# Decoder layer on one core: GpSimd's scaling and adding handed to VectorE, 16 bias adds made one, the last pair's weight sums moved into the up projection

## The chip, the cores and the metric

The kernel runs on one core of a Trainium2 chip. The metric is the device time of one execution in microseconds (us). The five engines of the core run their own instruction queues in order: TensorE (PE in the profile; its weight loads are PEld), VectorE (DVE), ScalarE (ACT), GpSimd (POOL) and SyncE (SP), which here only issues DMAs. Engines wait for each other through semaphores.

## The reference

One post-norm decoder layer in float32: 512 tokens, 1024 channels, 8 + 8 attention heads of 64, 2816 channels in the gated MLP. Cut to what matters here:

```python
mod = c @ w_ada + b_ada                      # six vectors of 1024
sh1, sc1, gt1, sh2, sc2, gt2 = split(mod, 6)
u = x * (1.0 + sc1) + sh1
q_a, k_a, v_a, f_a, q_b, k_b, v_b, g_a, g_b = split(u @ w_in)
y_fox = forgetting_attention(q_a, k_a, v_a, log_sigmoid(f_a + b_forget))
y_sb = stick_breaking_attention(q_b, k_b, v_b)
merged = sigmoid(g_a) * (y_fox @ w_fox_proj) + sigmoid(g_b) * (y_sb @ w_sb_proj)
x = layer_norm(ALPHA * x + (1.0 + gt1) * (merged @ w_o), ln1_g, ln1_b)
u2 = x * (1.0 + sc2) + sh2
h_gate, h_val = split(causal_depthwise_conv(u2 @ w_up, conv_w, conv_b), 2)
x = layer_norm(ALPHA * x + (1.0 + gt2) * ((silu(h_gate) * h_val) @ w_down), ln2_g, ln2_b)
```

## The kernel before

**Numbers.** Every large product is made in three matmuls of a float32 form (`wh*ah + wh*al + wl*ah`): an operand `r` is split into a rounded high part (`hi_of`, a copy on ACT, line 89) and the rest (`lo_of`, a subtraction on DVE, line 92). So each weight tile of 128x1024 costs an ACT copy and a DVE subtraction (`wl`, two inputs in SBUF) before PE can use it.

**The stream of weights.** `items` is one list of weight loads in the order of use. `weights(i)` issues loads through SP up to five items ahead (`LOADS = 5` buffers called `raw`) and runs each item's `proc` up to some items ahead of its use; the split products `wh`/`wl` have three buffers (`WBUFS = 3`). A load can start only when the last reader of its `raw` buffer is done. The order of instructions on all engines but SP is set by a scheduler at build time from this program order; SP's order is as written.

**Stages.** To 190 us: the first projections and the attention pairs, with the loads of `w_ada` in between (`ada_proc`). A `w_ada` block of 128x1024 is multiplied by `c` and summed along its row by one DVE instruction with an accumulator (`mod_sum`, line 201), and a bias is added to the one resulting column (`mod_col`, line 207, 128x1): `n` from 8 to 23 are the shift and scale of the MLP, which are first read at lines 845 to 847 (`gm`, `bm`, at 338 us). From about 244 to 345 us: the branch projections (`bproj`), the gates and the loads of `w_o`. `merge` adds the two gated branch sums on GpSimd (line 738, 128x512, eight times), and `wo_proc` multiplies each `w_o` block by `1 + gt1` on GpSimd (line 634, 128x1024, eight times) ahead of the split. From 345 to 372 us: the output projection and the first layer norm.

**Up projection and MLP** (372 to 674 us). 44 column blocks `n` of `w_up`, 24 matmuls of 512 columns each; after every fourth one, a pair `p = 0..10` of 256-channel groups of the hidden layer is complete. The down projection is a Strassen-Winograd scheme over 2x2 blocks, seven products per pair: the DVE makes sums of the activations (`blocks`, lines 1063 to 1066) and of the weights (`pair_proc`). For a pair, `raw` B is loaded (columns 0 to 1023 of `wdp[p]`) and columns 512 to 1535 are added to it by a GpSimd DMA; then the sums R are loaded (columns 1024 to 2047) and DVE makes `wg = R[0:512]*g` (line 946), `R[0:512] += B[0:512]` (947), `R[512:] += R[0:512]` (948), splits both halves of R (`wdc_proc`: `wdh`, `wdl`) and scales B by `g` (951). B goes to DRAM in `t13[p]`, `wg` in `wgt[p]`, both issued by ACT, and are loaded again in the phases after the up projection. `early_products(p)` makes three of the products with the halves of `wdp[p]` and the sums R; it stands behind block `n = 4p + 7`, for the last two pairs behind block 43 and in `z_mark`. `ready(p)` splits another sum of the activations into halves `hv` (two ACT copies and two DVE subtractions of 128x256); it is called in the up projection for the first `GS = 9` pairs and in `z_mark` for the rest.

**The last pair** (`p = 10`) is outside this pattern: its B, its halves and R are loaded behind the first Z load, its sums are made after block 43, B isn't stored but split from SBUF (`state["t13"]`), and `phase` uses that split in a special case (`last`).

**After the up projection:** four phases of products over the eleven pairs, Z (`zi`: `t13[p]` columns 512 to 1023), V (`vi`: `t13[p]` columns 0 to 511), X (`xi`) and W (`wi`, `cli`), each with two PSUM banks and with layer-norm work on DVE between them, then the tail.

Of the kernel before, what the change touches and what calls it, by code (L numbers as in the profile page):

```python
# [16 lines left out]
P = 128  # L17
# [25 lines left out]
GS = 9  # L43
# [8 lines left out]
def layer_kernel(ctx: ExitStack, tc: tile.TileContext, out, xT, x, cT, crow, wa0, wa1, bcol, bgt, w1, wct, wv, bf,  # L52
# [6 lines left out]
    t13 = [tc.dram_tile([P, 1024], F32, name=f"t13_{p}") for p in range(FP - 1)]  # L59
    wgt = [tc.dram_tile([P, 512], F32, name=f"wgt_{q}") for q in range(FP)]  # L60
    st1 = ExitStack()
# [571 lines left out]
    def wo_proc(r):  # L633
        G.tensor_tensor(r, r, gt[0], ALU.mult)  # L634
# [101 lines left out]
    def merge(j):  # L736
        def f(m):
            G.tensor_tensor(m, m, ma[j], ALU.add)
# [105 lines left out]
    bm = const([P, KT], F32, "bm")  # L844
    V.scalar_tensor_tensor(gm, lnc[:, 0, :], -0.5, modc[:, 3, :], ALU.mult, ALU.mult)
# [95 lines left out]
    def pair_proc(p):  # L941
        def f(r):
# [25 lines left out]
    wui, pi, wai = [], [], {}  # L968

    def add_pair_items(p):  # L970
        pi.append([add_item(wdp[p][:, 0:1024], raw_proc)])
        items[-1].append(wdp[p][:, 512:1536])
        pi[p].append(add_item(wdp[p][:, 0:512], halves_proc))

    def add_pair_sums(p):
        pi[p].append(add_item(wdp[p][:, 1024:2048], pair_proc(p)))

    for n in range(2 * FT):
# [206 lines left out]
    def phase(ps, idx, end, take, mark, last=None, fresh=True):  # L1185
# [7 lines left out]
        if end < FP:  # L1193
            t = take(end)
            for i in range(2):
                product(ps[i], t[:, top[i]], t[:, bot[i]], *[v[last] for v in state["t13"]], False, True)
            mark(len(idx))
# [57 lines left out]
    phase(Z, zi, FP - 1, g_part(0), z_mark, 1)  # L1255
    W1 = [bank() for _ in range(2)]
    phase(W1, vi, FP - 1, g_part(1), v_mark, 0)
# [100 lines left out]
```

## Time and profile before

| | us |
|---|---|
| median of 3 runs (lowest, highest) | 751.56 (750.51, 752.71) |
| profiled execution: time | 750.47 |
| profiled execution: span on the core | 748.7 |
| PE busy | 734.3 (98%) |
| DVE busy | 607.9 (81%) |
| ACT busy | 389.0 (52%) |
| POOL busy | 111.1 (15%) |

The profiled execution lasted 1.77 us longer than its span and 1.09 us less than the median of the runs. PE's granted clock is full over the whole span. A PE row's duration contains the drain of the matmul, so that a matmul of 512 columns shows 0.39 us while the next one starts after 0.23; a true stall is read from the start of one matmul to the start of the next. In the rows, an engine's idle time stands in square brackets with what ended it.

### The profile page before, as it was taken

The numbers are of one execution on the slowest core, as the hardware profiler recorded it, in microseconds if no ns is written. First come the engines' busy times: TensorE is split into PE (matmuls) and PEld (weight loads), VectorE is DVE, ScalarE is ACT, GpSimd is POOL, SyncE is SP. The second block draws the span as 40 slices with busy tenths as digits, with TensorE's granted clock in tenths as the row PEclk, the third lists the DMA queues.
The fourth block names the chain that finished last, engine by engine and source line by source line (L and its number), as shares of the span: only waits on it lengthen the run. The fifth ranks groups of instructions, "written<-read, shape, count | busy, mean of one in ns | idle before, by whom it ended". The sixth has DMA issues, their size and how long they took to land.

```text
span 748.7 us, 9890 instructions
## 1 busy us (share of the span) xinstructions
PE 734.3 (98%) x3478; PEld 608.1 (81%) x3478; DVE 607.9 (81%) x1018; ACT 389.0 (52%) x682; POOL 111.1 (15%) x140
## 2 busy tenths in 40 slices
PE   8999999999999999999999999999999999999995
PEld 4878888878888888788889888888888888887885
DVE  6869799888788795756577899988888696668996
ACT  4566465685876564443055455444454454436550
POOL 1026223353000011444000000000000000000010
PEclk9999999999999999999999999999999999999999
DMA  8943545413412230552052788577787574666734
GB/s 330 406 179 113 169 170 190 148 58 113 170 62 109 93 133 28 197 200 87 1 205 93 219 294 263 165 221 231 255 283 224 179 213 146 203 169 209 241 90 94
DMA packets 44244, 130.11 MB, mean 174 GB/s; under 512 B 5761, under 2 KB 6273, under 8 KB 44194
## 3 DMA queue, kind: packets, MB, share of 16 engines
q1 hardware_dynamic: 37890, 112.61, 43.1%
q0 software_dynamic: 2992, 7.93, 6.1%
q10 hardware_dynamic: 3312, 8.93, 3.2%
q8 instruction: 27, 0.44, 0.2%
q14 instruction: 23, 0.19, 0.1%
HBM read 117.59 MB, written 11.80 MB: 173 GB/s over the span
## 4 chain that ended last, share of the span: by engine, by line
PE 86%; DVE 7%; DMA 3%; ACT 2%; issue 2%; POOL 0%; SPq 0%; DVEq 0%; ACTq 0%
PE ps L136 18%; PE ps L134 18%; PE ps L135 18%; PE ps L302 5%; PE ps L1084 4%; PE ps L1082 4%; PE ps L1083 4%; PE ps L553 2%; PE ps L535 2%; PE ps L895 2%; PE ps L893 2%; PE ps L894 2%; DVE wl L92 1%; PE ps L476 1%; PE ps L477 1%
## 5 line engine op out<-in xcount | busy, mean ns | idle before, releaser
L92 DVE TENSOR_TENSOR wl<-raw,wh 128x1024 fp32r<-128x1024 f32 (+2 forms) x112 | 139.0, 1242 | 39.5 <-ACT wh L183 39.1
L183 ACT ACTIVATE wh<-raw 128x1024 fp32r<-128x1024 f32 (+1 forms) x103 | 108.3, 1052 | 108.2 <-PE ps L135 50.7
L134 PE MATMUL ps<-u2h,wh 128*128 128x512 f32 (+1 forms) x376 | 141.4, 376 | 0.0
L135 PE MATMUL ps<-u2l,wh 128*128 128x512 f32 (+1 forms) x376 | 141.2, 376 | 0.0
L136 PE MATMUL ps<-u2h,wl 128*128 128x512 f32 (+1 forms) x376 | 141.2, 375 | 0.0
L136 PEld LDWEIGHTS ps<-u2h,wl 128*128 128x128 f32 x376 | 70.8, 188 | 12.9
L135 PEld LDWEIGHTS ps<-u2l,wh 128*128 128x128 f32 x376 | 70.8, 188 | 12.8
L134 PEld LDWEIGHTS ps<-u2h,wh 128*128 128x128 f32 x376 | 70.8, 188 | 12.7
L134 PE MATMUL ps<-uh,wh 128*128 128x512 f32 x200 | 79.5, 397 | 0.0
L136 PE MATMUL ps<-uh,wl 128*128 128x512 f32 x200 | 78.3, 391 | 0.9 <-DVE wl L92 0.9
L135 PE MATMUL ps<-ul,wh 128*128 128x512 f32 x200 | 78.3, 391 | 0.0
L1132 ACT ACTIVATE cv<-ps,cw 128x512 f32<-128x512 f32 x44 | 34.0, 773 | 39.9 <-PE ps L136 30.7
L1133 DVE SCALAR_TENSOR_TENSOR cv<-ps,cw,cv 128x511 f32<-128x511 f32 x44 | 32.7, 744 | 15.6 <-ACT cv L1132 15.6
L136 PEld LDWEIGHTS ps<-uh,wl 128*128 128x128 f32 x200 | 37.6, 188 | 9.5 <-DVE wl L92 1.3
L515 POOL TENSOR_TENSOR pt<-pt,om 128x127 f32<-128x127 f32 (+3 forms) x32 | 43.2, 1361 | 8.0 <-DVE om L514 8.0
L134 PEld LDWEIGHTS ps<-uh,wh 128*128 128x128 f32 x200 | 37.6, 188 | 7.3
L135 PEld LDWEIGHTS ps<-ul,wh 128*128 128x128 f32 x200 | 37.6, 188 | 7.2
L162 POOL DMA_DIRECT2D raw<-in_wdp x11 | 9.6, 869 | 192.6 <-DVE raw L948 67.3
L1134 DVE SCALAR_TENSOR_TENSOR cv<-ps,cw,cv 128x510 f32<-128x510 f32 x44 | 32.7, 743 | 0.3
L1140 ACT ACTIVATE cv<-cv 128x512 f32<-128x512 f32 x22 | 13.9, 631 | 36.0 <-DVE cv L1134 36.0
L634 POOL TENSOR_TENSOR raw<-raw,gt 128x1024 f32<-128x1024 f32 x8 | 20.5, 2562 | 67.6 <-DMA raw<-in_wo 55.1
L514 DVE TENSOR_TENSOR_SCAN om<-om,dg 128x127 f32<-128x127 f32 (+3 forms) x32 | 29.6, 981 | 0.5 <-ACT om L509 0.4
(227 smaller groups left out, 1613.8 us busy)
## 6 DMA issues: line engine op xcount, KB each, us to landing
raw<-in_wup SPq DMA_DIRECT2D x44, 512.0 KB, 4.7
raw<-in_wa SPq DMA_DIRECT2D x32, 512.0 KB, 4.2
raw<-in_wct SPq DMA_DIRECT2D x25, 512.0 KB, 3.7
raw<-in_wdp SPq DMA_DIRECT2D x22, 512.0 KB, 5.4
wa<-in_wa SPq DMA_DIRECT2D x14, 512.0 KB, 7.6
raw<-in_wdp SPq DMA_DIRECT2D x22, 256.0 KB, 4.4
raw<-in_wdp POOLq DMA_DIRECT2D x11, 512.0 KB, 7.5
t<-raw ACTq DMA_DIRECT2D x10, 512.0 KB, 3.0
```

The costliest lines, as they stand in the source:

```text
L92: state["read"] = V.tensor_tensor(o, i, fl(hi), ALU.subtract)
L134: PE.matmul(ps, wh, ah, start=first, stop=False)
L135: PE.matmul(ps, wh, al, start=False, stop=False)
L136: return PE.matmul(ps, wl, ah, start=False, stop=last)
L183: state["hi"] = S.activation(h[:, 0:cols], r[:, 0:cols], AF.Copy)
L302: PE.matmul(grp[g], w, u, start=j == 0 and n == 0, stop=j == KT - 1 and n == (1 if g == 7 else 2))
L515: G.tensor_tensor(pt[b][:, s : e - 1], pt[b][:, s : e - 1], om[:, s + 1 : e], ALU.mult)
L1082: PE.matmul(ps, ah, bh, start=first, stop=False, skip_group_check=onto)
L1083: PE.matmul(ps, ah, bl, start=False, stop=False, skip_group_check=onto)
L1132: S.activation(t, ps, AF.Identity, bias=cw[:, n, 3:4], scale=cw[:, n, 2:3])
L1133: V.scalar_tensor_tensor(t[:, 1:], ps[:, 0:511], cw[:, n, 1:2], t[:, 1:], ALU.mult, ALU.add)
L1134: V.scalar_tensor_tensor(t[:, 2:], ps[:, 0:510], cw[:, n, 0:1], t[:, 2:], ALU.mult, ALU.add)
```

## The change

Four things are edited. (1) `ada_proc` calls only `mod_sum` for `n` from 8 to 23, so that the 16 one-column adds of line 207 are gone; one 128x16 add in front of `gm` (line 846 of the changed kernel) makes all 16 columns at once. (2) The eight multiplications of `wo_proc` and the eight additions of `merge` are issued on VectorE instead of GpSimd. (3) The last pair's B and R are loaded and summed as items behind blocks 31 and 32 of the up projection. R isn't split there but stored to a new DRAM tile `t24`, and B is stored to `t13[10]`; after the up projection the halves of `wdp[10]` and `t24` are loaded and split behind the first Z load, and `t13[10]` is the eleventh entry of the Z and V phases, whose special case goes. (4) `GS` is 7 instead of 9: `ready(7)` and `ready(8)` are called in `z_mark`.

```diff
-GS = 9
+GS = 7
...
-    t13 = [tc.dram_tile([P, 1024], F32, name=f"t13_{p}") for p in range(FP - 1)]
+    t13 = [tc.dram_tile([P, 1024], F32, name=f"t13_{p}") for p in range(FP)]
+    t24 = tc.dram_tile([P, 1024], F32, name="t24")
...
             if 8 <= n < 24:
-                mod_col(2 + (n - 8) // 8, n % 8, r)
+                mod_sum(2 + (n - 8) // 8, n % 8, r, slice(0, D), 0)
                 return
...
     def wo_proc(r):
-        G.tensor_tensor(r, r, gt[0], ALU.mult)
+        V.tensor_tensor(r, r, gt[0], ALU.mult)
...
         def f(m):
-            G.tensor_tensor(m, m, ma[j], ALU.add)
+            V.tensor_tensor(m, m, ma[j], ALU.add)
...
+    V.tensor_tensor(modc[:, 2:4, :], modr[:, 2:4, :, 0], bcols[:, 2:4, :], ALU.add)
     V.scalar_tensor_tensor(gm, lnc[:, 0, :], -0.5, modc[:, 3, :], ALU.mult, ALU.mult)
...
-            w = wdc_proc(r)
+            w = wdc_proc(r) if p < FP - 1 else None
...
             with tc.issue_after(state["last"].ins):
-                if p < FP - 1:
-                    S.dma_start(t13[p], b)
+                S.dma_start(t13[p], b)
                 if p > 1:
                     S.dma_start(wgt[p], g)
-            if p == FP - 1:
-                state["t13"] = wdc_proc(b)
+                if p == FP - 1:
+                    S.dma_start(t24, r)
             return w
...
+        if n == 31:
+            add_pair_items(FP - 1)
+        if n == 32:
+            add_pair_sums(FP - 1)
...
-    for p in range(0, FP - 1, 2):
-        add_two(zi, lambda q: t13[q][:, 512:1024], p, FP - 1)
+    for p in range(0, FP, 2):
+        add_two(zi, lambda q: t13[q][:, 512:1024], p, FP)
         if p == 0:
-            add_pair_items(FP - 1)
-            add_pair_sums(FP - 1)
-    for p in range(0, FP - 1, 2):
-        add_two(vi, lambda q: t13[q][:, 0:512], p, FP - 1)
+            pi[FP - 1].append(add_item(wdp[FP - 1][:, 0:512], halves_proc))
+            pi[FP - 1].append(add_item(t24, wdc_proc))
+    for p in range(0, FP, 2):
+        add_two(vi, lambda q: t13[q][:, 0:512], p, FP)
```

The order of the instructions, at the three places of which the prediction speaks. First VectorE in the attention stage, from the scans `om` of the stick-breaking branch to the forget gate's row `fq`; `m` and `pl` are low parts of attention operands, `wl` of a weight tile. Before:

```order
L514 SCALAR_TENSOR_TENSOR om_1582<-om_1582,dg 128x511
L92 TENSOR_TENSOR wl_1618<-raw_1609,wh_1617 128x1024
L207 TENSOR_TENSOR modc<-modr,bcols 128x1
L92 TENSOR_TENSOR m_0_553<-ps_1528,m_300_1597 64x512
L92 TENSOR_TENSOR m_1_554<-ps_1528,m_301_1600 64x512
L92 TENSOR_TENSOR pl_1633<-ps_1627,ph_1632 128x512
L92 TENSOR_TENSOR pl_1641<-ps_1636,ph_1640 128x384
L92 TENSOR_TENSOR ptc_544<-ps_1644,ptc_543 128x384
L359 SCALAR_TENSOR_TENSOR fq_571<-fq_571,fq_570 8x512
L360 SCALAR_TENSOR_TENSOR fq_570<-ones,fq_571 8x512
```

and in the changed kernel:

```order
L515 SCALAR_TENSOR_TENSOR om_1580<-om_1580,dg 128x511
L93 TENSOR_TENSOR wl_1616<-raw_1607,wh_1615 128x1024
L93 TENSOR_TENSOR m_0_555<-ps_1527,m_300_1595 64x512
L93 TENSOR_TENSOR m_1_556<-ps_1527,m_301_1598 64x512
L93 TENSOR_TENSOR pl_1631<-ps_1625,ph_1630 128x512
L93 TENSOR_TENSOR pl_1639<-ps_1634,ph_1638 128x384
L93 TENSOR_TENSOR ptc_546<-ps_1642,ptc_545 128x384
L360 SCALAR_TENSOR_TENSOR fq_573<-fq_573,fq_572 8x512
L361 SCALAR_TENSOR_TENSOR fq_572<-ones,fq_573 8x512
L93 TENSOR_TENSOR wl_1682<-raw_1609,wh_1681 128x1024
```

The 128x1 add between `wl` and `m` is gone, and nothing else moves.

Second VectorE where the branch sums (`sg`, `ml`), the `w_o` blocks (`woh`, `wol`) and the gates' weights (`wl`) meet. Before:

```order
L207 TENSOR_TENSOR modc<-modr,bcols 128x1
L628 TENSOR_TENSOR sg_2948<-ps_3117,sg_2948 128x512
L92 TENSOR_TENSOR wl_3150<-raw_3139,wh_3149 128x1024
L92 TENSOR_TENSOR ml_3133<-sg_2948,mh_3132 128x512
L92 TENSOR_TENSOR wl_3194<-raw_3180,wh_3193 128x1024
L92 TENSOR_TENSOR wol_3187<-raw_3141,woh_3185 128x512
L92 TENSOR_TENSOR wl_3230<-raw_3216,wh_3229 128x1024
L92 TENSOR_TENSOR wol_3188<-raw_3141,woh_3186 128x512
L628 TENSOR_TENSOR sg_3021<-ps_3179,sg_3021 128x512
L92 TENSOR_TENSOR ml_3212<-sg_3021,mh_3211 128x512
```

and in the changed kernel, where L739 is the branch sum, L635 the scaling of a `w_o` block and L846 the one bias add:

```order
L846 TENSOR_TENSOR modc<-modr,bcols 128x16
L629 TENSOR_TENSOR sg_2937<-ps_3104,sg_2937 128x512
L93 TENSOR_TENSOR wl_3136<-raw_3126,wh_3135 128x1024
L739 TENSOR_TENSOR sg_2937<-sg_2937,sg_653 128x512
L635 TENSOR_TENSOR raw_3128<-raw_3128,gt_1210 128x1024
L93 TENSOR_TENSOR ml_3120<-sg_2937,mh_3119 128x512
L93 TENSOR_TENSOR wl_3180<-raw_3166,wh_3179 128x1024
L635 TENSOR_TENSOR raw_3168<-raw_3168,gt_1210 128x1024
L93 TENSOR_TENSOR wol_3173<-raw_3128,woh_3171 128x512
L93 TENSOR_TENSOR wl_3216<-raw_3202,wh_3215 128x1024
L93 TENSOR_TENSOR wol_3174<-raw_3128,woh_3172 128x512
L629 TENSOR_TENSOR sg_3009<-ps_3165,sg_3009 128x512
```

A branch sum and two scalings now stand in VectorE's queue there, the first of them between `wl_3136` and `ml_3120`.

Third the last pair. SyncE's loads around blocks 32 to 35 of the up projection, before:

```order
L157 DMA raw_5587<-in_wup 128x1024
L157 DMA raw_5589<-in_wup 128x1024
L157 DMA raw_5591<-in_wup 128x1024
L157 DMA raw_5635<-in_wdp 128x1024
L157 DMA raw_5638<-in_wdp 128x512
L157 DMA raw_5698<-in_wup 128x1024
L157 DMA raw_5744<-in_wdp 128x1024
L157 DMA raw_5807<-in_wup 128x1024
L157 DMA raw_5809<-in_wup 128x1024
L157 DMA raw_5811<-in_wup 128x1024
```

and in the changed kernel, where `raw_5576` is B of the last pair and `raw_5623` its R:

```order
L158 DMA raw_5574<-in_wup 128x1024
L158 DMA raw_5576<-in_wdp 128x1024
L158 DMA raw_5579<-in_wup 128x1024
L158 DMA raw_5623<-in_wdp 128x1024
L158 DMA raw_5625<-in_wup 128x1024
L158 DMA raw_5693<-in_wdp 128x1024
L158 DMA raw_5696<-in_wdp 128x512
L158 DMA raw_5738<-in_wup 128x1024
L158 DMA raw_5740<-in_wdp 128x1024
L158 DMA raw_5801<-in_wup 128x1024
L158 DMA raw_5803<-in_wup 128x1024
L158 DMA raw_5805<-in_wup 128x1024
```

Each of the two stands between loads of `w_up`, so that the `w_up` blocks behind them take `raw` buffers that come free later. VectorE after block 43, before, from the last pair's first weight sum to the halves `hv` for its early products:

```order
L946 TENSOR_TENSOR wg_6383<-raw_6273,gt_4554 128x512
L92 TENSOR_TENSOR wl_6442<-raw_6380,wh_6441 128x1024
L947 TENSOR_TENSOR raw_6273<-raw_6273,raw_6235 128x512
L92 TENSOR_TENSOR wl_6479<-raw_6405,wh_6478 128x1024
L948 TENSOR_TENSOR raw_6273<-raw_6273 128x512
L92 TENSOR_TENSOR wdl_6389<-raw_6273,wdh_6387 128x512
L951 TENSOR_TENSOR raw_6235<-raw_6235,gt_4554 128x512
L92 TENSOR_TENSOR wdl_6390<-raw_6273,wdh_6388 128x512
L92 TENSOR_TENSOR wl_6507<-raw_6438,wh_6506 128x1024
L92 TENSOR_TENSOR wdl_6399<-raw_6235,wdh_6397 128x512
L92 TENSOR_TENSOR wdl_6400<-raw_6235,wdh_6398 128x512
L92 TENSOR_TENSOR hv_6432<-cv_6162,hv_6432 128x256
```

and in the changed kernel:

```order
L93 TENSOR_TENSOR wl_6387<-raw_6370,wh_6386 128x1024
L1074 TENSOR_TENSOR sg_1191_6359<-cv_6150,cv_6253 128x256
L93 TENSOR_TENSOR wl_6412<-raw_6373,wh_6411 128x1024
L93 TENSOR_TENSOR fo_6365<-cv_6150,fh_6364 128x256
L93 TENSOR_TENSOR fo_6365<-cv_6253,fh_6364 128x256
L93 TENSOR_TENSOR hv_6402<-cv_6150,hv_6402 128x256
L93 TENSOR_TENSOR hv_6405<-cv_6253,hv_6405 128x256
L93 TENSOR_TENSOR hv_6445<-sg_1062_5687,hv_6445 128x256
L93 TENSOR_TENSOR hv_6448<-sg_1062_5687,hv_6448 128x256
L93 TENSOR_TENSOR wl_6455<-raw_6376,wh_6454 128x512
```

The four sums of lines 946 to 951 and the four `wdl` are gone from there (two `wdl` of `t24` stand earlier), and the halves `hv_6445` and `hv_6448` of pair 7 (`ready`) have come in.

More of the change, by code (lines that the diff above doesn't have):

```diff
@@ L966, in scale_proc @@
         return f
-    wui, pi, wai = [], [], {}
+    wui, pi, wai = [], [[] for _ in range(FP)], {}
     def add_pair_items(p):
-        pi.append([add_item(wdp[p][:, 0:1024], raw_proc)])
+        pi[p].append(add_item(wdp[p][:, 0:1024], raw_proc))
         items[-1].append(wdp[p][:, 512:1536])
-        pi[p].append(add_item(wdp[p][:, 0:512], halves_proc))
+        if p < FP - 1:
+            pi[p].append(add_item(wdp[p][:, 0:512], halves_proc))
     def add_pair_sums(p):
-        pi[p].append(add_item(wdp[p][:, 1024:2048], pair_proc(p)))
+        n = add_item(wdp[p][:, 1024:2048], pair_proc(p))
+        if p < FP - 1:
+            pi[p].append(n)
     for n in range(2 * FT):
@@ L1183, in layer_kernel, with phase @@
     p1, u2, q1, u3, tm = [[fine(n) for _ in range(2)] for n in ("p1", "u2", "q1", "u3", "tm")]
-    def phase(ps, idx, end, take, mark, last=None, fresh=True):
+    def phase(ps, idx, end, take, mark, fresh=True):
         for n, k in enumerate(idx):
@@ L1192, in phase @@
             mark(n)
[L1193 to L1197, printed above, removed]
     def g_part(c):
@@ L1254, in layer_kernel @@
     Z = [bank() for _ in range(2)]
-    phase(Z, zi, FP - 1, g_part(0), z_mark, 1)
+    phase(Z, zi, FP, g_part(0), z_mark)
     W1 = [bank() for _ in range(2)]
-    phase(W1, vi, FP - 1, g_part(1), v_mark, 0)
+    phase(W1, vi, FP, g_part(1), v_mark)
     phase(P1, xi, FP, lambda p: ops[p][1], x_mark, fresh=False)
```

## The prediction

> **What bounds the kernel now.** I read the page's first part, then PE's waits, then a table by stage (after the span: busy time and count of PE, PEld, DVE, ACT and POOL, then PE's clock, DMA share and GB/s), and last the timeline around each wait. All numbers are of the one profiled execution: 750.47 us, which is 748.7 of span and 1.77 around it, and 1.09 below the median of 751.56.
>
> ```profile
> PE 734.3 (98%) x3478; PEld 608.1 (81%) x3478; DVE 607.9 (81%) x1018; ACT 389.0 (52%) x682; POOL 111.1 (15%) x140
> ...
> PE ps L553 <- DVE m L92: 0.9, 1, 0.9
> PE ps L136 <- DVE wl L92: 0.9, 1, 0.9
> PE ps L1084 <- DVE hv L92: 0.6, 1, 0.6
> ...
> 293.00:316.00 23.00, 22.12 (x100) 17.88 (x99) 16.23 (x19) 11.43 (x17) 8.65 (x4) 1.00 0.45 161
> 316.00:365.00 49.00, 49.00 (x218) 40.55 (x217) 28.16 (x37) 15.23 (x24) 18.50 (x10) 1.00 0.32 110
> 540.00:610.00 70.00, 70.00 (x311) 57.93 (x310) 55.63 (x89) 34.27 (x55) 3.16 (x4) 1.00 0.69 221
> 666.00:693.00 27.00, 25.75 (x109) 19.70 (x108) 22.39 (x37) 15.10 (x26) 0.00 (x0) 1.00 0.55 188
> 693.00:735.00 42.00, 42.00 (x188) 34.76 (x188) 39.30 (x67) 20.63 (x30) 3.51 (x4) 1.00 0.59 159
> ```
>
> PE is the bound: 98% busy at full clock (the 1.00). So work that is added to DVE or taken from POOL changes nothing by itself; only PE's stalls do, and they are few and short. In 540 to 610 us 311 matmuls fill 70.00 us, 0.225 each; at that pace the 109 matmuls of 666 to 693 need 24.5 of the 27.00, so about 2.5 us are lost there. The three waits in the list are the three places that the change touches.
>
> **Part 1, the 16 adds.** First PE's rows at the stall of line 553 and at the next one, then DVE's, ACT's, and two pieces of the chain of waits between them:
>
> ```profile
> 157.67 0.39 PE L453 MATMUL ps<-wh,ul 128*128 128x512 f32 x1
> 158.95 0.65 PE L553 MATMUL ps<-ph,vv 128*128 128x512 f32 x2 [0.89 <-DVE m L92]
> ```
>
> ```profile
> 186.25 0.52 PE L535 MATMUL ps<-ident,pt 128*128 128x128 f32 x3 [0.37 <-DVE vv L92]
> ```
>
> ```profile
> 156.36 1.04 DVE L207 TENSOR_TENSOR modc<-modr,bcols 128x1 f32<-128x1 f32 x1
> 157.41 1.39 DVE L92 TENSOR_TENSOR m<-ps,m 64x512 fp32r<-64x512 f32 x2
> ...
> 160.42 0.68 DVE L359 SCALAR_TENSOR_TENSOR fq<-fq,fq 8x512 f32<-8x512 f32 x1
> ```
>
> ```profile
> 159.76 0.63 ACT L358 ACTIVATE fq<-fq 8x512 f32<-8x512 f32 x1
> ```
>
> ```profile
> 163.49 3.36 DMA raw<-in_wa
> ...
> 173.94 4.45 DMA raw<-in_wa
> ```
>
> The 128x1 add takes 1.04 us here, in front of the `m` for which PE waits. Without it `m` starts 1.04 earlier, and PE's 1.28 from start to start (157.67 to 158.95) falls to the pace of 0.23: the stall of 1.05 goes. But what is late next? ACT's `fq` ends at 160.39, and DVE's line 359, which reads it, started at 160.42: from there on DVE keeps its old times, whatever it gained. The next weight tile frees the buffer for the load issued at 163.49, whose block is summed before the scans; these and the next tile set the load at 173.94; its sum stands before the `vv` for which PE waits at 186.25. The chain from 160 to 186 runs over DVE and two loads and not over PE, so PE arrives 1.05 earlier at 186.25 and waits there. What remains is the adds on that chain and the 0.03 at `fq`, one or two adds of 0.07 to 0.16 as rows: I take −0.2. The bounds are 0 and −1.05 (the chain moves with PE). The new 128x16 add has 16 times the columns of an add that is nearly all fixed cost; it runs once, at about 306 us, and counts below.
>
> **Part 2, POOL's work on DVE.** DVE's rows at the stall of line 136, and POOL's around it:
>
> ```profile
> 309.45 2.22 DVE L92 TENSOR_TENSOR ml<-sg,mh 128x512 fp32r<-128x512 f32 x1 [1.84 <-ACT mh L89]
> 311.60 3.44 DVE L92 TENSOR_TENSOR wl<-raw,wh 128x1024 fp32r<-128x1024 f32 x1
> ```
>
> ```profile
> 306.56 2.19 POOL L738 TENSOR_TENSOR sg<-sg,sg 128x512 f32<-128x512 f32 x1 [5.93 <-DVE sg L628]
> 308.72 5.24 POOL L634 TENSOR_TENSOR raw<-raw,gt 128x1024 f32<-128x1024 f32 x2
> 318.06 1.29 POOL L738 TENSOR_TENSOR sg<-sg,sg 128x512 f32<-128x512 f32 x1 [4.10 <-DVE sg L628]
> 322.72 3.24 POOL L634 TENSOR_TENSOR raw<-raw,gt 128x1024 f32<-128x1024 f32 x1 [3.37 <-DMA raw<-in_wo]
> ```
>
> DVE's prices with POOL idle, 0.68 for 128x512 and 1.21 for 128x1024 (rows of the last pair's sums and of the W phase), and PE's first use of that W tile:
>
> ```profile
> 685.06 0.68 DVE L947 TENSOR_TENSOR raw<-raw,raw 128x512 f32<-128x512 f32 x1
> ...
> 724.92 1.21 DVE L92 TENSOR_TENSOR wl<-raw,wh 128x1024 fp32r<-128x1024 f32 x1
> ```
>
> ```profile
> 726.31 0.40 PE L1083 MATMUL ps<-wl,hv 128*128 128x512 f32 x1
> ```
>
> DVE gets 8 × 1.21 + 8 × 0.68 = 15.1 us over some 75 us. It gets time back where an operation of its own was stretched while POOL worked: `ml` by 2.22 − 0.68, `wl` by 3.44 − 1.21, together 3.8 us in 293 to 316, as much as the two scalings and two sums that come in there. With POOL's work gone the queue at the stall runs so: POOL's branch sum of 306.56 could start when `sg` was done; on DVE a tile stands ahead of it (1.21), then the sum (0.68), a scaling (1.21) and `ml` (0.68), which ends at 310.3. The `wl` behind it starts between that and 311.60, since ACT's half of it was ready by then (the row names no wait), and ends by 312.8 instead of 315.04. PE asked for it 0.9 before 315.04, at about 314.1. So that stall goes too: 0.88 by PE's idle time in the table, 1.04 with the drain of the last matmul (above, 1.05 against 0.89). PE has no idle time in 316 to 365 nor in 540 to 610 and no listed wait until 666, so it isn't handed on: −1.0; bounds 0 and −1.05. Where a scaling now waits in DVE's queue for its load (POOL waited 3.37 before 322.72), the branch sums and tiles behind it wait too; what hides it is that PE is 49.00 busy of 49.00 in 316 to 365 while DVE has 20.8 us free there. I cost it at nothing; if the cover is gone, it is rival B.
>
> The Trainium skill, page Perfetto Trace Analysis, section Optimizing Scalar/DVE Operations, speaks against this part: when DVE is saturated it advises offloading to ScalarE or even GpSimd, with the caveat that GpSimd and DVE share an SBUF read port. By the advice rival B is the case, by the caveat this sum; the stretched rows bear out the caveat.
>
> **Part 3, the last pair.** From behind block 43 DVE loses four sums and two splits of 0.68, 4.1 us; it gains four `hv` of 128x256 for `ready(7)` and `ready(8)` and two 128x512 tiles for `t13[10]`. By the two prices a column costs 0.53/512 us and an operation 0.15, so an `hv` 0.42: 4 × 0.42 + 2 × 0.68 = 3.0. That makes 1.1 us less before the W phase, but all 4.1 less before the early products of the last pair, where line 1084 waits. Walking the new order, most of the 2.5 goes and some 0.6 remain (PSUM banks of blocks 42 and 43, and `hv`; an estimate between 0 and 1.5). But in 693 to 735 DVE is busy 39.30 of 42.00; the first tile of W ends at 724.92 + 1.21 = 726.13 and PE uses it at 726.31. So PE can come only as much earlier as DVE does, 1.1, plus one 128x512 statistics operation (0.68 by size) that the new order puts behind this tile. I take −1.7; bounds −0.4 (half of the wait of line 1084 and its drain) and −2.5.
>
> In the up projection the four sums of the last pair (2.7 us) fit into a wait of DVE. The transfers are the doubtful point:
>
> ```profile
> raw<-in_wup SPq DMA_DIRECT2D x44, 512.0 KB, 4.7
> ...
> t<-raw ACTq DMA_DIRECT2D x10, 512.0 KB, 3.0
> ```
>
> ```profile
> 597.39 1.23 DVE L92 TENSOR_TENSOR wl<-raw,wh 128x1024 fp32r<-128x1024 f32 x1 [4.21 <-ACT wh L183]
> ...
> 609.75 1.28 DVE L92 TENSOR_TENSOR wdl<-raw,wdh 128x512 fp32r<-128x512 f32 x2
> ```
>
> ```profile
> 612.87 0.39 PE L1083 MATMUL ps<-wdl,fh 128*128 128x512 f32 x1
> ```
>
> Two items take a `raw` buffer out of turn and hold it until a store has ended. The last pair's sums end by 597.4 (inside the 4.21); the store to `t24` then takes 3.0 and the load of pair 7's R into that buffer 4.7, so it lands near 605. On DVE follow four sums (2.7), two splits (1.4) and about two weight tiles between them (2.4), which is 611.5, and up to 614 with their waits for ACT's halves; today the splits end at 611.0, and PE reads them from 612.87. That is late by 0 to 1: +0.3, with the bounds 0 and +2. The later loads of `t24` and `t13[10]` replace loads of the same size.
>
> Sum: −0.2 − 1.0 − 1.7 + 0.3 = −2.6, so 747.9 for a run like the profiled one, and **749.0** against the median. The tail behind 735 us keeps its work.
>
> **Rivals.** A, slower: the last pair's loads and stores starve PE in the up projection. SP and ACT move 1.5 MB of loads earlier and store 1.25 MB, 2.75 MB in about 33 us, 83 GB/s on top of what stands in the slices (18.7 us each) around 590:
>
> ```profile
> GB/s 330 406 179 113 169 170 190 148 58 113 170 62 109 93 133 28 197 200 87 1 205 93 219 294 263 165 221 231 255 283 224 179 213 146 203 169 209 241 90 94
> ```
>
> These are 179 and 213 (the 32nd and 33rd), so 262 to 296, which the 30th slice carried at 283 without a stall of PE. For it speaks that pair 7 has none: every us by which its store and load take longer than 3.0 + 4.7 is a stall before its early products. It decides when they take 5.1 us longer (12.8): 2.9 of gains eaten and 2.25 lost, time 753.8 or more. The page DMA: Bandwidth & Descriptors of the Trainium skill, section Issuing engines are not separate DMA queues, says that all engines' transfers interleave on the same 16 DMA engines. By it ACT's stores slow SP's loads and A gains; the slice at 283 GB/s shows no harm yet.
>
> B, slower: a scaling waits at the head of DVE's queue for its `w_o` load and the gate tiles behind it come late. Price up to the wait that POOL shows at 322.72, 3.37 per load, less what DVE's free 20.8 us cover; three such loads uncovered cost 10. It decides when half of that reaches PE (5.1, as in A): 753.8.
>
> C: the stall before the W phase grows as the one at 666 to 693 shrinks, and part 3 brings 0.3: −0.9, time 750.7. For it speaks that DVE has no gap there.
>
> D: the chain up to 186 us moves with PE after all, and part 1 brings its 1.05: 748.1. Against it stands the row of `fq`.
>
> That the edits act at all is not in doubt for 1 and 2: the stretched rows name them.
>
> **Chances.** The forecast 0.48 (range of its own 748.0 to 750.2, of which 0.32 is faster by over 0.3%, that is below 749.3, and 0.16 within); D 0.18, faster; C 0.16, within; A 0.12 and B 0.06, slower. A difference of 0.3% (2.25 us) is about what a measurement of this kernel can tell from none. Faster 0.50, same 0.32, slower 0.18. The range, 746.9 to 753.0, takes in at the low end D with all of the 2.5 and nothing lost in the up projection (−1.05 − 1.0 − 2.5 = −4.6), and at the high end the near half of A and B.
>
> **What the profile after would show.** Part 1: no wait at line 553, a longer one for `vv` at 186. Part 2: no wait of L136 near 314, `wl` at 1.21 everywhere from 270 to 345, DVE's rows waiting for `raw<-in_wo`. Part 3: no DVE sums after 680, a wait at pair 7's early products near 612 of at most 0.8, and W's first tile as the next late one. I am wrong if PE waits for `wl` in 590 to 625, or if DVE waits for `w_o` loads while PE idles.

## The result and the profile after

| | before | after |
|---|---|---|
| median (lowest, highest), 11 runs each, us | 750.79 (750.34, 752.71) | 749.23 (747.66, 751.27) |
| ratio, 95% interval | | 0.9982 [0.9974, 0.9989] |
| profiled execution: time, span, us | 750.47, 748.7 | 749.85, 748.1 |

The change is worth 0.18%, some 1.35 us. The interval leaves out 1, but the difference is below the 0.3% that the prediction took for the least that a measurement of this kernel can tell from none. First, of the kernel after: the page's busy times, then PE's waits, then the stages that the prediction named (after the span: busy time and count of PE, PEld, DVE, ACT and POOL; PE's clock, DMA share, GB/s).

```profile
PE 733.7 (98%) x3478; PEld 608.6 (81%) x3478; DVE 608.1 (81%) x1019; ACT 389.5 (52%) x682; POOL 79.0 (11%) x124
```

```profile
PE ps L1091 <- DVE wdl L93: 1.2, 1, 1.2
PE ps L536 <- DVE vv L93: 1.2, 2, 0.7
PE ps L477 <- DVE m L93: 0.6, 1, 0.6
```

```profile
150.00:190.00 40.00, 38.84 (x196) 32.14 (x195) 32.34 (x50) 28.09 (x54) 16.82 (x26) 1.00 0.26 87
293.00:316.00 23.00, 23.00 (x105) 18.94 (x104) 18.43 (x26) 11.54 (x17) 0.00 (x0) 1.00 0.45 161
316.00:365.00 49.00, 49.00 (x218) 40.60 (x217) 30.14 (x46) 15.42 (x24) 0.00 (x0) 1.00 0.32 110
590.00:625.00 35.00, 33.60 (x146) 26.94 (x145) 23.75 (x38) 13.91 (x22) 1.72 (x2) 1.00 0.70 208
666.00:693.00 27.00, 26.84 (x119) 21.90 (x118) 21.78 (x39) 15.77 (x30) 0.00 (x0) 1.00 0.61 206
693.00:735.00 42.00, 42.00 (x191) 34.96 (x190) 38.09 (x64) 20.05 (x27) 3.50 (x4) 1.00 0.58 150
```

The same number of matmuls is made by a PE that runs at full clock in both profiles, so the accounts can be kept in matmuls per stage, 0.225 us each. In 293 to 316 PE makes 105 where it made 100 (1.1 us won), in 666 to 693 it makes 119 where it made 109 (2.25 won). The two gains come to 3.4 us. In 590 to 625 it makes 146; before it made 156 there:

```profile
590.00:625.00 35.00, 35.00 (x156) 28.99 (x155) 25.86 (x41) 14.88 (x24) 0.86 (x1) 1.00 0.56 180
```

Those ten are 2.25 us lost. And in 150 to 190 the count is 196 in both. What is left, about 1.1 us, is what PE's rows show: its last matmul ends at 739.88 instead of 740.96. The spans of the two profiled executions differ by 0.6 only, as the tail behind that matmul took 8.2 us instead of 7.7; the medians differ by some 1.35. In what follows, "lost" in a stage means the same thing counted more finely: the sum, over all matmuls of the stage, of the time from one start to the next beyond the usual fast pace of that kind of matmul. It is read from one profiled execution of each kernel. By it the kernel before loses 2.47, 1.40, 0.11 and 2.76 us in 150–190, 293–316, 590–625 and 660–693, the kernel after 2.51, 0.23, 2.40 and 0.56.

So the question is where the 2.3 us at pair 7 come from, and why the first edit brought nothing. The chain of waits of the kernel after, from the last pair's stores to the early products of pair 7 (start, length, what), and PE's rows at its end:

```profile
594.17 7.29 DMA t<-raw
601.60 4.72 DMA raw<-in_wup
606.35 1.07 ACT wh L184
607.44 0.90 DVE wl L93
...
610.91 1.22 DVE wl L93
612.13 0.60 DVE raw L950
612.74 0.60 DVE wdl L93
```

```profile
611.72 0.51 PE L1090 MATMUL ps<-wdh,fh 128*128 128x512 f32 x1
613.39 0.50 PE L1091 MATMUL ps<-wdl,fh 128*128 128x512 f32 x1 [1.17 <-DVE wdl L93]
```

The store of 512 KB to `t13[10]` takes 7.29 us (issued at 594.17, after the one to `t24` at 593.57). The load that takes over its buffer is a weight tile of the up projection and takes 4.72. Its split (`wl` at 607.44) stands ahead of pair 7's sums and splits in DVE's queue, so that `wdl` is done at 613.3. PE's two matmuls there start 1.68 apart, 1.45 more than usual; the rest of the 2.3 lost are gaps of 0.1 to 0.4 before and behind it. SyncE's own waits between 588 and 606 us, the longest in total of each kernel, say the same: it waits for the two stores that have not left their buffers. First the kernel before, where no wait for a store is listed there, then after (total, times, longest):

```profile
SPq L157 <- DVE wl L92: 15.8, 3, 6.0
```

```profile
SPq L158 <- DMA t<-raw: 7.8, 2, 6.9
```

### The profile page after: what moved, and what is told of

Read it like the earlier page. It is cut to its first block, busy times and chain, and to the rows that moved or that the text cites. A ratio compares the mean times of both kernels' runs of the same rounds, so it can differ in the third digit from the quotient of the medians.

```text
span 748.1 us, 9865 instructions
## 1 busy us (share of the span) xinstructions
PE 733.7 (98%) x3478; PEld 608.6 (81%) x3478; DVE 608.1 (81%) x1019; ACT 389.5 (52%) x682; POOL 79.0 (11%) x124
## 4 chain that ended last, share of the span: by engine, by line
PE 90%; DMA 4%; DVE 3%; ACT 1%; issue 1%; SPq 0%; ACTq 0%; DVEq 0%
PE ps L135 18%; PE ps L136 18%; PE ps L137 18%; PE ps L303 5%; PE ps L1090 4%; PE ps L1092 4%; PE ps L1091 4%; PE ps L554 3%; PE ps L536 2%; PE ps L896 2%; PE ps L895 2%; PE ps L897 2%; PE ps L453 2%; PE ps L452 2%; PE ps L454 2%; PE ps L477 1%
## 5 line engine op out<-in xcount | busy, mean ns | idle before, releaser
L93 DVE TENSOR_TENSOR wl<-raw,wh 128x1024 fp32r<-128x1024 f32 (+2 forms) x114 | 135.4, 1189 | 37.6 <-ACT wh L184 37.0
L135 PE MATMUL ps<-u2h,wh 128*128 128x512 f32 (+1 forms) x376 | 141.5, 376 | 0.0
L135 PEld LDWEIGHTS ps<-u2h,wh 128*128 128x128 f32 x376 | 70.8, 188 | 12.8
L136 PEld LDWEIGHTS ps<-u2l,wh 128*128 128x128 f32 x376 | 70.8, 188 | 12.8
L135 PE MATMUL ps<-uh,wh 128*128 128x512 f32 x200 | 79.5, 397 | 0.0
L135 PEld LDWEIGHTS ps<-uh,wh 128*128 128x128 f32 x200 | 37.6, 188 | 7.4
L1090 PE MATMUL ps<-wh,hv 128*128 128x512 f32 x72 | 28.1, 390 | 0.2 <-DVE cv L1142 0.2
```

The source lines that it names most:

```text
L93: state["read"] = V.tensor_tensor(o, i, fl(hi), ALU.subtract)
L135: PE.matmul(ps, wh, ah, start=first, stop=False)
L136: PE.matmul(ps, wh, al, start=False, stop=False)
L1090: PE.matmul(ps, ah, bh, start=first, stop=False, skip_group_check=onto)
```

## The experiments

Each kernel is compared with the kernel before, run beside it on the same chip.

**The three parts, one at a time.** The kernel before with only the first edit (e1), only the second (e2), only the third and fourth (e3, of whose diff the core is shown).

```diff
# e1
-                mod_col(2 + (n - 8) // 8, n % 8, r)
+                mod_sum(2 + (n - 8) // 8, n % 8, r, slice(0, D), 0)
...
+    V.tensor_tensor(modc[:, 2:4, :], modr[:, 2:4, :, 0], bcols[:, 2:4, :], ALU.add)
# e2
-        G.tensor_tensor(r, r, gt[0], ALU.mult)
+        V.tensor_tensor(r, r, gt[0], ALU.mult)
...
-            G.tensor_tensor(m, m, ma[j], ALU.add)
+            V.tensor_tensor(m, m, ma[j], ALU.add)
# e3
-GS = 9
+GS = 7
...
+        if n == 31:
+            add_pair_items(FP - 1)
+        if n == 32:
+            add_pair_sums(FP - 1)
...
+                if p == FP - 1:
+                    S.dma_start(t24, r)
```

> The kernel before with the 16 bias adds made one, alone. Theory (the 1.05 us stall before line 553 at 157 us goes, but the chain up to 186 us runs over two loads and VectorE, so that PE waits longer for vv there): 0 to -0.3 us against the kernel before, PE's wait for vv at 185 us grows from 0.4 to about 1.2 us in all. Rival (the chain moves with PE): -1.05 us and the wait for vv stays at 0.4.

> The kernel before with the eight w_o scalings and the eight branch sums on VectorE, alone. Theory (the stall of 1.04 us at 314 us goes and is handed on to nothing): -1.0 us (-0.7 to -1.2), no wait of PE between 293 and 365 us. Rival (VectorE's queue waits for w_o loads): 0 or slower, with PE waiting for wl between 316 and 345 us.

> The kernel before with the last pair's sums in the up projection and GS = 7, alone. Theory (2.2 us won at 666 to 693 us, 2.3 us lost before pair 7's early products at 612 us): within 0.5 us of the kernel before, and both seen in the stages. Rival (the stall at 612 us comes from the other two parts, by which PE arrives earlier there): -1.5 to -2.2 us, with less than 0.8 us lost at 612.

| | median, us | ratio, 95% interval | lost 150–190 | 293–316 | 590–625 | 660–693 |
|---|---|---|---|---|---|---|
| e1 | 750.46 | 0.9999 [0.9990, 1.0008] | 2.29 | 1.46 | 0.10 | 2.96 |
| e2 | 749.72 | 0.9987 [0.9979, 0.9996] | 2.55 | 0.23 | 0.10 | 2.97 |
| e3 | 750.20 | 0.9992 [0.9982, 1.0003] | 2.84 | 1.56 | 2.05 | 0.68 |

Each part moves its own stage and no other of these four by more than 0.4 us. Part 2 by itself brings nearly what the whole change brings. In the kernel after, the `wl` that took 3.44 us beside GpSimd's work is this row:

```profile
310.50 1.23 DVE L93 TENSOR_TENSOR wl<-raw,wh 128x1024 fp32r<-128x1024 f32 x1 [0.54 <-ACT wh L184]
```

Part 3 wins 2.1 us at one end and loses 1.9 at the other. Part 1 removes its stall and wins nothing: DVE's rows of e1 show the work behind the removed add starting earlier and then waiting for ACT.

```profile
156.05 1.39 DVE L92 TENSOR_TENSOR m<-ps,m 64x512 fp32r<-64x512 f32 x2
157.47 1.16 DVE L92 TENSOR_TENSOR pl<-ps,ph 128x512 fp32r<-128x512 f32 x2
158.54 0.55 DVE L92 TENSOR_TENSOR ptc<-ps,ptc 128x384 fp32r<-128x384 f32 x1
160.01 0.68 DVE L359 SCALAR_TENSOR_TENSOR fq<-fq,fq 8x512 f32<-8x512 f32 x1 [0.93 <-ACT fq L358]
```

**Does DVE's chain with its two loads decide the time at 186 us?** e11 is e1 with the two row sums of `w_ada` blocks at 167 and 178 us left out (two columns of the MLP's shift are left without their sum), so that nothing on that chain waits for these loads or works on them.

```diff
         def f(r):
+            if n in (13, 14):
+                return
             if 8 <= n < 24:
```

> The run with the 16 adds made one, in which VectorE also leaves out the two w_ada row sums that stand at 167 and 178 us (two columns of the MLP's shift are then left without their sum; their loads are still made, a GpSimd memset at the start gives the columns a value). Theory (those sums wait for their loads in VectorE's queue and hold back vv at 185 us, which ate part 1's gain): PE's wait for vv falls from 1.0 to below 0.4 us, and -1.0 to -1.5 us against the kernel before. Rival (vv is late for another reason, ScalarE's or GpSimd's): the wait stays at 0.8 us or more, within 0.4 us of the kernel before.

750.13 us, ratio 0.9990 [0.9981, 0.9999]; lost in 150–190: 0.95 where e1 lost 2.29. PE's waits in e1 and in e11, behind the longest, which is the same in both:

```profile
...
PE ps L535 <- DVE vv L92: 1.0, 2, 0.7
PE ps L136 <- DVE wl L92: 0.9, 1, 0.9
```

```profile
...
PE ps L137 <- DVE wl L92: 0.9, 1, 0.9
PE ps L1088 <- DVE hv L92: 0.6, 1, 0.6
```

The wait for `vv` is gone, so it does hang on DVE's chain with the loads, and this chain is what held the gain of the first edit back. In e1 DVE waits 4.5 us in all for the two loads, and the sums themselves are 2.6 us of its work; e11 takes both away, so it does not tell the waiting from the work. Of the 1.34 us won there, about 0.5 are lost again between 450 and 540 us (0.81 where e1 loses 0.28; e4 below, which has both sums, loses 0.97 there) and 0.2 in 660–693; why was not followed up. In the whole time e1 and e11 are not told apart: their intervals overlap.

**Is it the buffers held, or the bytes?** e4 lets the last pair's sums write tiles of their own, from which they are stored, so that the `raw` buffers come free as soon as DVE and ACT have read them (one ACT copy is added). e5 leaves the two stores out at this place and stores the same number of bytes of another tile at block 14 (the last pair's part of the output is not computed).

```diff
# e4, against the kernel after
+            if p == FP - 1:
+                r0, r1, b0, b1 = [z(F32, "lp") for _ in range(4)]
+                V.tensor_tensor(r0, r[:, 0:512], b[:, 0:512], ALU.add)
+                state["read"] = V.tensor_tensor(r1, r[:, 512:1024], r0, ALU.add)
+                V.tensor_tensor(b0, b[:, 0:512], gt[1][:, 512:1024], ALU.mult)
+                S.activation(b1, b[:, 512:1024], AF.Copy)
+                with tc.issue_after(state["last"].ins):
+                    S.dma_start(wgt[p], g)
+                    for e, (x, y) in enumerate(((r0, b0), (r1, b1))):
+                        c = slice(e * 512, (e + 1) * 512)
+                        S.dma_start(t24[:, c], x)
+                        S.dma_start(t13[p][:, c], y)
+                return None
# e5, against the kernel after
-                S.dma_start(t13[p], b)
+                if p < FP - 1:
+                    S.dma_start(t13[p], b)
...
-                if p == FP - 1:
-                    S.dma_start(t24, r)
...
+        if n == 14:
+            S.dma_start(t24, gt[1])
+            S.dma_start(t13[FP - 1], gt[1])
```

> The changed kernel, in which the last pair's sums are written to four tiles of their own (one half of B by an added ScalarE copy) and stored from there, so that its two raw buffers are free when VectorE and ScalarE have read them and not when the stores have landed; the bytes moved are the same. Theory (the held buffers make the stall at 612 us): the stall of 2.3 us there falls below 0.5 us, -1.8 to -2.3 us against the changed kernel, about -3.5 against the kernel before. Rival (the transfers themselves are too many there, or VectorE's four added sums are in the way): the stall stays, within 0.5 us of the changed kernel.

> The changed kernel without the two stores of the last pair's sums (0.5 MB each) behind block 32; in their place the same bytes are stored from another tile at block 14, so that the later loads stay as they are. What the two tiles then hold is not the last pair's sums, so that this pair's part of the result is left out. Theory (the stores' traffic and the buffers that they hold, together, make the stall of 2.3 us at 612 us): below 0.6 us lost between 590 and 625, -1.8 to -2.3 us against the changed kernel. Rival (the earlier loads of B and R, or the four sums in VectorE's queue, make it): at least 1.5 us are still lost there.

e4: 750.18 us, ratio 0.9999 [0.9988, 1.0009], 2.16 lost in 590–625. e5: 747.61 us, ratio 0.9956 [0.9939, 0.9973], 0.05 lost. e5 keeps the earlier loads of B and R and the four sums on DVE, so these are not the cause: without the two stores nothing is lost. "Held buffers alone" fell as well. In e4 the loads are issued at once, and one of them takes 8.69 us with the stores beside it; the same load takes 6.1 us in e5 (issued at 593.97) and 5.9 in e10 below (594.84), where no such store runs beside it. The chain of waits of e4, then ACT's rows at its end:

```profile
595.62 8.69 DMA raw<-in_wup
```

```profile
604.39 1.06 ACT L184 ACTIVATE wh<-raw 128x1024 fp32r<-128x1024 f32 x1 [3.10 <-DMA raw<-in_wup]
605.36 0.76 ACT L1153 ACTIVATE cv<-ps,cw 128x512 f32<-128x512 f32 x1
```

ACT waits at the weight tile's copy for that load, and the `cv` behind it, which empties a PSUM bank, is late for the matmuls (`PE ps L135 <- DVE cv L1155`, 1.8 us). The place of the wait changed, its size hardly. Stores of this stretch in the kernel after (three of 512 KB, shortest, median and longest), in e4 and in e5 (count, KB each, median us from issue to landing):

```profile
DMA to landing us min/median/max: 6.7/7.3/9.1
```

```profile
t<-lp ACTq DMA_DIRECT2D x4, 256.0 KB, 8.3
```

```profile
t<-raw ACTq DMA_DIRECT2D x1, 512.0 KB, 2.9
```

In e5 the one store of 512 KB (at 607.43) takes 2.9 us. In the kernel after, the two issued 0.6 us apart take 6.7 and 7.3, and the third, issued alone at 613.97 but among loads, 9.1; the four halves of 256 KB in e4 have a median of 8.3. So it is not the second store as such that makes a store slow, but what is in flight beside it. The page DMA: Bandwidth & Descriptors of the Trainium skill, section Issuing engines are not separate DMA queues, has the transfers of all engines interleave on the same 16 DMA engines; the runs agree, whether the store or the load is the one that is stretched.

**Another place.** e6 puts the last pair behind blocks 35 and 36, e7 behind 39 and 40.

```diff
# e6
-        if n == 31:
+        if n == 35:
             add_pair_items(FP - 1)
-        if n == 32:
+        if n == 36:
             add_pair_sums(FP - 1)
```

> The changed kernel with the last pair's loads and sums behind blocks 35 and 36 instead of 31 and 32. Theory (too many transfers at once around 590 to 606 us, where the page shows 0.84 DMA share just before): the same traffic meets a quieter stretch (0.63 of the DMA engines after 625), and less than 1.0 us is lost in 590 to 666 instead of 2.4; -1.4 us or more against the changed kernel. Rival (the stall belongs to the order of the loads and hits the pair that follows, here pair 8): 1.8 to 2.5 us are lost before pair 8's early products at about 640, same time.

> The changed kernel with the last pair's loads and sums behind blocks 39 and 40. Theory (traffic): less than 1.0 us lost in 590 to 666, but the sums' stores come close to the loads of the Z phase at 664, so that up to 1 us may be lost in 666 to 693: -1 to -2 us against the changed kernel. Rival (order of the loads): about 2 us lost before pair 9's early products at about 665.

e6: 752.73 us, ratio 1.0021 [1.0006, 1.0035], 5.63 lost in 625–660. e7: 748.78 us, ratio 0.9974 [0.9965, 0.9983], nothing lost in 590–660, 2.56 in 660–693. The idea of a quieter place fell: the loss goes along to the next pair (in e7 PE waits at 662.87, before pair 9's early products). In e6 ACT's rows, and PE's behind them:

```profile
631.19 1.06 ACT L184 ACTIVATE wh<-raw 128x1024 fp32r<-128x1024 f32 x1 [6.05 <-DMA raw<-in_wup]
632.15 0.76 ACT L1140 ACTIVATE cv<-ps,cw 128x512 f32<-128x512 f32 x1
```

```profile
631.25 0.39 PE L137 MATMUL ps<-u2h,wl 128*128 128x512 f32 x1
635.30 0.47 PE L135 MATMUL ps<-u2h,wh 128*128 128x512 f32 x1 [3.66 <-DVE cv L1142]
...
636.67 0.63 PE L137 MATMUL ps<-u2h,wl 128*128 128x512 f32 x1
```

Again the evacuation of a PSUM bank stands in ACT's queue behind a copy that waits for a load. After this wait matmuls follow each other at 0.43 us for eight of them: PE's clock was lowered. This comes back below.

**Spread the stores.** e10 is e4 with its four stores of 256 KB issued one by one, each behind ACT's first read of one of the blocks 35 to 38.

```diff
-                    for e, (x, y) in enumerate(((r0, b0), (r1, b1))):
-                        c = slice(e * 512, (e + 1) * 512)
-                        S.dma_start(t24[:, c], x)
-                        S.dma_start(t13[p][:, c], y)
+                state["lp"] = [(t24[:, 0:512], r0), (t24[:, 512:1024], r1), (t13[p][:, 512:1024], b1), (t13[p][:, 0:512], b0)]
...
-        S.activation(t, ps, AF.Identity, bias=cw[:, n, 3:4], scale=cw[:, n, 2:3])
+        ev = S.activation(t, ps, AF.Identity, bias=cw[:, n, 3:4], scale=cw[:, n, 2:3])
+        if n in (35, 36, 37, 38):
+            with tc.issue_after(ev.ins):
+                S.dma_start(*state["lp"].pop(0))
```

> As the run with four tiles of their own, but the four stores of 0.25 MB are issued one by one behind ScalarE's first read of blocks 35, 36, 37 and 38 instead of all behind block 32. Same bytes, same loads, same sums. Theory (two stores of 0.5 MB on top of the loads of blocks 34, 35 and pair 7 make these land late, whichever way the buffers are freed): below 0.8 us lost in 590 to 625, -1.5 to -2.3 us against the changed kernel, about 747.5. Rival (the out-of-turn loads and ScalarE's order make the stall, or it follows the stores to pair 8): 1.5 us or more are lost in 590 to 666.

747.20 us, ratio 0.9953 [0.9940, 0.9965], some 2.2 us (0.9953 against 0.9982) faster than the changed one. It leaves nothing out, and no kernel here that does so is faster. Its row for 590 to 625:

```profile
590.00:625.00 35.00, 35.00 (x156) 29.00 (x155) 27.75 (x43) 14.89 (x23) 1.72 (x2) 1.00 0.73 223
```

All 156 matmuls are back, with more bytes per second than the kernel after moves there (223 against 208), so the mean rate of a stage doesn't tell what it costs. What is gone is the stores beside the loads of 593 to 602 us that someone waits for: e10 issues its four at 620.54, 627.34, 634.97 and 639.65, and they take 2.0 to 8.2 us without a matmul being late for them (0.1 lost in 625–660). They are later as well as spread; e6, whose two stores of 512 KB are issued together at 616.68 and 617.29, loses 5.63 there, but its loads stand elsewhere too, and four stores issued together at e10's place were not tried.

**`GS`.** e9 is the kernel before with `GS = 7`, e8 the kernel after with `GS = 9`, e12 is e10 with `GS = 9`.

```diff
-GS = 7
+GS = 9
```

> The kernel before with GS = 7 and nothing else. Theory (the handover's gain needs both, the last pair's sums gone from behind block 43 and room for them by GS): within 0.7 us of the kernel before, 2.0 us or more still lost in 666 to 693. Rival (GS alone brings the gain, since GS = 9 costs the changed kernel 3.8 us): -1.5 to -2.2 us, less than 1.0 us lost there.

> The changed kernel with GS = 9 as before. Theory (the last pair's sums, gone from behind block 43, bring the 2.2 us of the handover; GS moves 1.5 us of VectorE's work out of a stretch in which it is nearly full, to the up projection): within 0.5 us of the changed kernel. Rival (GS brings the handover's gain): 1 to 2 us slower than the changed kernel, lost in 666 to 693.

> e10's kernel with GS = 9: the sums of pairs 7 and 8 are split in the up projection again, all else as e10 (stores of the last pair one by one behind the convolution of blocks 35 to 38). In e8 PE lost 4.24 us in 590 to 625 and 4.36 in 660 to 693, each time with waits of over 2.3 us from start to start and then eight matmuls at 0.43 us instead of 0.23. Theory 'ACT's order': in e8 ACT's first copy of block 43 and the hv that PE needs stood behind a weight tile's copy that waited 5.90 us for a load of t, so the stall near 669 has nothing to do with the stores; it stays here with its slow matmuls (3 to 4.4 us lost in 660 to 693) while 590 to 625 loses nothing: 749.3 to 751.5 us, ratio 0.998 to 1.001. Theory 'transfers': the load of t is late because the stores of the last pair pushed everything back; then 660 to 693 loses under 1 us and the time is that of e10, 747.0 to 748.0, ratio 0.995 to 0.997.

| | median, us | ratio, 95% interval | lost 590–625 | 660–693 |
|---|---|---|---|---|
| e9 | 751.31 | 1.0008 [0.9998, 1.0017] | 0.10 | 3.00 |
| e8 | 753.01 | 1.0040 [1.0025, 1.0056] | 4.24 | 4.36 |
| e12 | 751.12 | 1.0000 [0.9988, 1.0013] | 0.10 | 4.35 |

By itself `GS` brings nothing; with the last pair moved it decides between a gain and a loss. e8 came out slower than either of its two expectations had it. In e12 the stores do no harm and the stall in 660–693 is the same as in e8, so the stores aren't its cause. ACT's rows at that place, with `GS = 7` (e10) and with `GS = 9` (e12):

```profile
660.79 0.78 ACT L1150 ACTIVATE cv<-ps,cw 128x512 f32<-128x512 f32 x1 [0.31 <-issue]
661.47 0.41 ACT L90 ACTIVATE hv<-cv 128x256 fp32r<-128x256 f32 x1
666.52 1.06 ACT L184 ACTIVATE wh<-raw 128x1024 fp32r<-128x1024 f32 x1 [4.64 <-DMA raw<-t]
```

```profile
665.95 1.06 ACT L184 ACTIVATE wh<-raw 128x1024 fp32r<-128x1024 f32 x1 [5.95 <-DMA raw<-t]
666.91 0.76 ACT L1150 ACTIVATE cv<-ps,cw 128x512 f32<-128x512 f32 x1
667.58 0.71 ACT L90 ACTIVATE hv<-cv 128x256 fp32r<-128x256 f32 x2
```

With `GS = 7` one `cv` and one `hv` stand ahead of the tile's copy that waits for a load of `t`; with `GS = 9` they stand behind it, and PE waits for `hv`. In the kernel before, where PE waits there for DVE's last sums and splits, either value loses about the same (2.76 and 3.00).

## Why the prediction was right, and where not

The forecast was 749.0 us against a median of 751.56, a gain of 2.6; measured are 749.23 against 750.79, a gain by the ratio of about 1.35. It lies in the range, and the sign is right, but the gain is half of the one forecast: one term was off by 2.0 us, more than the whole gain. That 749.0 and 749.23 lie so close is luck: the kernel before came out 0.8 lower in eleven runs than in the three that the forecast started from.

- **Part 1, −0.2.** Right: 0.0 in the profile of the change (2.47 against 2.51 lost) and 0.9999 in e1. The stall at 157.67 went, the wait for `vv` grew, as the row of `fq` had said; e11 shows that the chain with the two loads carries it. Rival D is out.
- **Part 2, −1.0.** Right: 1.17 won in the stage, ratio 0.9987 in e2. DVE's `wl` takes 1.23 instead of 3.44, and no wait for it is left. Rival B is out: one scaling waited 1.16 us for its `w_o` load, and PE stayed at 49.00 of 49.00 in 316 to 365.
- **The handover to the last phases, −1.7.** Measured −2.2 (2.76 to 0.56), near the bound of −2.5. The limit that I put before the W phase did not bind: PE has no wait there (42.00 of 42.00), and DVE starts the W tile at 721.71 instead of 724.92, 3.2 us earlier:

```profile
721.71 1.23 DVE L93 TENSOR_TENSOR wl<-raw,wh 128x1024 fp32r<-128x1024 f32 x1
```

  Of these, 1.1 and 0.68 were in the sum, and DVE's busy time from block 43's last `cv` to this tile bears them out (43.47 us instead of 45.29). The other 1.4 the sum did not have: DVE ends that `cv` 0.5 earlier (678.15 instead of 678.62) and waits 0.9 less on the way (0.1 instead of 1.0). Rival C is out.
- **The up projection, +0.3 with the bounds 0 and +2.** This is the step that failed: "the store to `t24` then takes 3.0 and the load of pair 7's R into that buffer 4.7, so it lands near 605". The 3.0 was the median of the stores of the kernel before, one per pair; two run together here, and took 6.7 (`t24`, 593.57 until SyncE could issue the next load at 600.29) and 7.29. Pair 7's R landed at 605.0 all the same, by luck: its store took 3.7 longer than in the sum and was issued 3.8 earlier than the 597.4 I had. What came late was the weight tile in the other buffer: I had put two such tiles into the sum as time on DVE (2.4), and not that the load of one waits for the second store (601.60 + 4.72). The first of the two splits, for which PE waited, ended at 613.3 and the second at 614.5, past my 611.5 to 614, and PE asked at 611.95 and not at 612.87, since part 2 had brought it forward; the wait is 1.17 where I had at most 0.8, and the loss is 2.3, a little above the upper bound. PE's coming earlier does not make the loss: in e3, without parts 1 and 2, PE asks at 612.98, the first split ends at 614.22, and 1.9 are lost. Rival A had named this mechanism; store and load came to 12.0 on this chain, short of the 12.8 at which I had it decide (by A's price of 1 us per us, these 12.0 would have cost 4.3), so the change stayed on the faster side with two thirds of its gain eaten (2.3 of 3.4). That a slice of 283 GB/s had passed without harm told nothing of A: e10 moves more than the kernel after and loses nothing.
- **`GS`, four `hv` at 0.42.** The price was right as DVE time and missed what the edit does. It keeps an `hv` ahead of a copy on ACT that waits for a load: worth some 3.5 us once the last pair is moved (0.9953 in e10 against 1.0000 in e12), nothing without it (e9). I costed the instructions that it moves and not the order on ACT's queue.

Open: how much of the 2.3 us is due to the held buffers by themselves. e4 frees them and wins nothing, as its loads are stretched instead; e10 frees them and issues the stores later and spread; stores spread with the buffers still held were not tried, nor stores that are later but together.

## What to carry to other kernels

The landing time of a transfer that an edit adds should be taken from rows where as much is in flight as there will be, not from the median of the page: the same 512 KB took 2.9 us in a quiet stretch, 7.3 beside a second store and 9.1 among loads. A store that nobody is waiting for can be cut into pieces and issued later, one by one, behind steps that come at PE's pace anyway. And when an edit moves loads, look on each in-order queue for what stands behind the instruction that waits for them: a copy on ACT that waits for its load holds up the emptying of PSUM banks and so PE.

## What the runs showed of the hardware that was not expected

PE's clock fell after waits of little over 2 us. In e12 PE stood from 665.63 to 668.03, and then:

```profile
665.63 0.39 PE L1101 MATMUL ps<-wdl,fh 128*128 128x512 f32 x1
668.03 0.75 PE L1100 MATMUL ps<-wdh,hv 128*128 128x512 f32 x1 [2.01 <-ACT hv L90]
668.58 0.63 PE L1101 MATMUL ps<-wdl,hv 128*128 128x512 f32 x1
669.01 0.63 PE L1100 MATMUL ps<-wdh,hv 128*128 128x512 f32 x1
```

```profile
664.70:668.11 3.41, 1.40 (x7) 0.83 (x5) 1.07 (x1) 2.16 (x4) 0.00 (x0) 1.00 0.86 326
668.11:671.52 3.41, 3.41 (x8) 2.69 (x9) 3.41 (x8) 1.15 (x3) 0.00 (x0) 0.50 0.49 154
```

The start of one matmul is 0.43 from the next instead of 0.23, the granted clock is 0.50, and it lasts for 3.41 us; eight matmuls at 0.2 us more are 1.6 us on top of the wait. This is why e6 and e8 lose so much more than their waits. It came after gaps of 2.35 us from start to start (e8, 669.30), 2.40 (e12) and 4.04 (e6), and after 1.19 and 1.68 that followed each other at once (e8, 610.97); not after 2.17 (e4), 1.68 (after), 1.40 (e7) or 1.26 and 1.34 at 683.36 and 684.96 (e9).

The length of the gap is not what decides. In all 14 traces each stretch of full clock up to a fall is a whole multiple of 3.413 us (658.77 in e12 is 193 of them, 628.05 in e6 is 184), and each stretch of half clock between two of full clock is exactly one. So the clock changes only on a grid of 3.413 us, whose place differs from execution to execution. Laid over PE's rows, the grid stretches just before the four falls inside PE's work have PE busy for 1.06 (e6), 1.40 (e12), 1.42 and 1.45 us (e8) of 3.41; the least busy one after which the clock stayed full has 1.64 (e7, from 737.61, where PE's work ends), and no stretch of the 14 traces contradicts a limit between the two. In e4 a boundary at 607.50 cuts the gap of 2.17 in two, and neither side falls below it:

```profile
604.08:607.50 3.42, 2.98 (x14) 2.13 (x12) 2.02 (x3) 2.04 (x3) 0.00 (x0) 1.00 0.60 241
607.50:610.91 3.41, 2.07 (x9) 1.75 (x10) 3.38 (x8) 2.00 (x3) 0.00 (x0) 1.00 0.49 156
```

So whether a stall of about 2 us costs 1.6 more depends on where it falls on the grid. The other executions of e4 fit this, though no trace of them was kept: in three of eleven the mean granted clock is 0.994 to 0.995 and the time 752.4 to 752.5 us, in the other eight, the profiled one among them, 0.996 to 0.998 and 749.1 to 751.0. The Trainium skill, page TensorE: Matmul & The Clock Gate, section Why this matters for your kernels, puts the limit at PE idle gaps of about 3 us, and half the clock after them: half the clock agrees with the 0.43, but three of the four falls here came after shorter gaps.
